# First products of 32 tokens by rows fetched by index, and dense weights scattered eight tokens at a time

## The chip, the core and the metric

The kernel runs on one core of a Trainium2 chip. A core has engines that work side by side, each with its own stream of instructions: TensorE (PE; its weight loads are listed apart as PEld), VectorE (DVE), ScalarE (ACT) and GpSimd (POOL). SyncE (SP) starts most transfers; 16 DMA engines carry them out between DRAM and the on-chip memories SBUF (operands) and PSUM (outcomes of TensorE). The metric is the device time of one run in microseconds (us). Before the change it was 1877.42 us, the median of 3 runs from 1877.06 to 1878.47.

## The reference, cut to what matters

One block of a hybrid network works on 512 tokens of 1024 features, with 16 meta tokens ahead of them: a norm, a recurrent branch and an attention branch, their gated sum with a residual, a second norm, and then a layer of 16384 small experts, of which every token takes 8 heads x 16 = 128. The change lies in that layer:

```python
def one_chunk(xt):                                   # 128 tokens
    q = (xt @ w_q).reshape(BLOCK, PEER_HEADS, PEER_QDIM)
    s1 = jnp.einsum('chd,nd->chn', q[..., :half], keys1)
    s2 = jnp.einsum('chd,nd->chn', q[..., half:], keys2)
    t1, i1 = lax.top_k(s1, PEER_TOPK)
    t2, i2 = lax.top_k(s2, PEER_TOPK)
    cand = (t1[..., :, None] + t2[..., None, :])     # 16 x 16 pairs of a head
    cidx = (i1[..., :, None] * PEER_NKEYS + i2[..., None, :])
    ts, sel = lax.top_k(cand, PEER_TOPK)             # the 16 best pairs
    idx = jnp.take_along_axis(cidx, sel, axis=-1)
    g = jax.nn.softmax(ts, axis=-1)
    act = jax.nn.gelu(jnp.einsum('chkd,cd->chk', u[idx], xt))
    return jnp.einsum('chk,chkd->cd', g * act, v[idx])
```

So a token's outcome is the sum over its 128 experts of weight x gelu(u[expert] . x) x v[expert]. The tables u and v have 16384 rows of 1024 numbers each. A last norm follows.

## The kernel before

The 512 tokens are four chunks of 128, taken in the order 1, 2, 3, 0 (`ORDER`). A float32 product is made of three products of split operands (`mm3`, L180 to 183): high by high, high by low, low by high, where ScalarE makes the high part (L155) and VectorE the low part (L156) of a weight tile (`wload`).

Chunk 0 goes by index: GpSimd fetches for each of 128 choices the 128 rows of u that the tokens want (`fetch`, L902), VectorE multiplies them by the tokens and sums each row (L913), and the same is done with v (L922).

Chunks 1 to 3, 384 tokens, go densely. For each of 128 blocks of 128 experts, `dense_products` makes `a` = u . x with 8 x 3 products of 384 columns, `gelu` makes `act` of it on ScalarE (L820), `stage` multiplies it by the dense softmax weights (`gt`, read from DRAM `gd`) and `dense` makes 18 products `y` of 512 columns with v, which sum up in PSUM over all blocks. First products run `LAG` = 41 blocks ahead of second products: block 0 within the mixing, 1 to 38 beside the choice and the scatter (`first_ahead`), and from block 39 on in the dense stage, where a step j holds the first products of block j + 41 and the second of block j. There a scheduler keeps VectorE's instructions in program order; elsewhere it places an instruction when its operands and a free buffer are there, earlier program order first. Pools with few buffers (`bufs`) tell when a transfer or an instruction can begin.

The dense weights come out of `scatter` (L843 to 881), once for each dense chunk. Its inputs are the choice's outcome `efx` (index) and `gate` (weight) of the chunk (`choose`, L757 to 815, nearly all on VectorE). After three transposes (`sct`) it goes four tokens at a time: VectorE makes `hb` (one-hot of the block, L868) and `hot` (one-hot of the expert within its block, L870); ScalarE scales three of four tokens' `hb` to `wj` (L875) and VectorE the fourth (L877); TensorE multiplies `hot` by `wj` into PSUM `sc` (L878); ScalarE copies `sc` to `stg` (L879), which holds 32 tokens. Every 32 tokens SyncE sends `stg` to `gd` (L881). The copy's loop is

```python
A.copy(stg[:, :, t4:t4 + 4].rearrange("p j t -> p t j"), o.rearrange("p (t j) -> p t j", t=4))
```

that is, it reads PSUM in order and writes with a distance of 32 numbers. The program's order (L883 to 890) is: key scores; choice of chunk 1; then three times a scatter in step with the next choice; each with its share of the blocks of `first_ahead`, by the table `ahead`.

Of the kernel before, what the change touches and what calls it, by code (L numbers as in the profile page):

```python
# [8 lines left out]
F32 = mybir.dt.float32  # L9
# [10 lines left out]
P = 128  # L20
D = 1024
NK = 8            # 128-row pieces of D_MODEL
NM = 16           # meta tokens
# [4 lines left out]
NH = 16           # attention heads  # L28
SCALE = 96.0 ** -0.5
PH = 8            # PEER heads  # L30
TOPK = 16
NS = PH * TOPK    # chosen experts of a token
NCAND = 50        # pairs (a, b) of ranks with (a + 1) * (b + 1) <= 16
NEG = -3.0e38
BIG = 1.0e30
# The pair of rank k (from 0) has (a + 1) * (b + 1) <= k + 1: blocks (a0, na, b0, nb) of pairs, by the
# group of four ranks that they can first have.
# [5 lines left out]
CO = (3, 0, 2, 1)    # chunks of queries of a pair of heads: the two sizes of the probabilities in turn  # L43
NJ = 128          # blocks of 128 experts
LAG = 41          # blocks that the first product runs ahead of the second
TS = 32           # tokens of a piece of the dense weights
JG = 4            # blocks of a load of the dense weights
# How the experts of a chunk are computed. Chunk 0: rows of both tables fetched by index.
# Chunks 1 to 3: products with both whole tables, times the dense softmax weights.
NDC = 3  # L50
ORD = (mybir.EngineType.DVE,)
SCA = 3           # tokens of four that ScalarE scales
LT = 2            # blocks of the first product between the two phases
GE = 6            # steps by which the fetches of rows end early
GA = ((0, 2), (2, 5))          # gate tiles that are computed between those of the recurrent branch
# [3 lines left out]
DT = NDC * P      # tokens of the dense chunks  # L59

# columns of the packed per-feature vectors
# [7 lines left out]
class in_order:  # L69
    """Keeps the instructions of the given engines that are traced within in the order of the program."""  # L70
# [22 lines left out]
def now(gen):  # L93
    """Runs a generator through; what it returns."""
    while True:
        try:
            next(gen)
        except StopIteration as e:
            return e.value
# [7 lines left out]
def interleave(*gens):  # L107
    """Runs generators in step, by the share of each that is done."""
# [10 lines left out]
def hybrid_block_kernel(ctx: ExitStack, tc, hT, x, win, wkr, vecs, wgate, wrnn, watt, wuq, wukv, wout,  # L119
# [9 lines left out]
    xn2d = dram.tile([P, D], F32, name="xn2d")  # L129
# [515 lines left out]
    def norm2(pos, c):  # L645
# [8 lines left out]
        if c == 0:  # L654
            nc.sync.dma_start(xn2d, t)
# [427 lines left out]
```

## Time and profile before

| | before |
|---|---|
| median of 3 runs | 1877.42 us (1877.06 to 1878.47) |
| profiled execution, its span | 1876.3 us |
| TensorE busy | 1821.0 us (97%) |
| VectorE busy | 1470.3 us (78%) |
| ScalarE busy | 981.4 us (52%) |
| GpSimd busy | 356.4 us (19%) |
| DMA, mean | 208 GB/s, 390.34 MB in all |

The trace is of one execution; its span is from its first to its last instruction, and 1.1 us lie between the span and the median of the runs. A busy share is a mean over stages with different limits, so the table below the change lists the stages apart: 553 to 688 us key scores, 688 to 717 the first choice, 717 to 967 the scatters and the other choices, 967 to 1697 the dense stage with both products, 1697 to 1822 its end with second products alone. Busy time of TensorE counts its matmuls with ends that are modelled, since they overlap.

### The profile page before, as it was taken

How to read it: one execution, taken by the hardware profiler on the slowest of the kernel's cores; microseconds unless marked ns; L12 is line 12 of the kernel's file. 1: busy time of each engine (PE TensorE's matmuls, PEld its weight loads, DVE VectorE, ACT ScalarE, POOL GpSimd, SP SyncE). 2: the span in 40 equal slices, each digit the busy share in tenths (PEclk: the TensorE clock that was granted, in tenths of full speed). 3: DMA queues.
4: the chain of work that ended last, by engine and by line, in shares of the span. 5: the costliest groups of instructions: out<-in, count | busy, mean ns of one | idle time of the engine just before them, and what ended most of it. 6: DMA issues, size and time to landing. Idle time of an engine off the chain costs nothing.

```text
span 1876.3 us, 28456 instructions
## 1 busy us (share of the span) xinstructions
PE 1821.0 (97%) x9731; PEld 1600.0 (85%) x9731; DVE 1470.3 (78%) x3280; ACT 981.4 (52%) x1915; POOL 356.4 (19%) x295
## 2 busy tenths in 40 slices
PE   8999999999999999999999999999999999999997
PEld 7888778877788888888899999998999999998886
DVE  7787677777546999898858788787887888887775
ACT  5778576766334337999963333333333333333343
POOL 0100000000100000000014344344444444443310
PEclk9999999999999999999999999999999999999999
DMA  5333212112733223454569999989998899988764
GB/s 162 92 101 104 74 54 66 62 55 85 241 113 129 85 85 130 144 194 158 189 225 348 321 318 340 326 300 322 324 334 313 304 331 321 343 309 280 266 223 152
DMA packets 181602, 390.34 MB, mean 208 GB/s; under 512 B 16593, under 2 KB 68305, under 8 KB 179921
## 3 DMA queue, kind: packets, MB, share of 16 engines
q1 hardware_dynamic: 141632, 245.97, 38.9%
q0 software_dynamic: 39536, 142.00, 21.8%
q8 instruction: 76, 1.25, 0.3%
q14 instruction: 70, 0.57, 0.1%
q10 hardware_dynamic: 288, 0.56, 0.1%
HBM read 353.44 MB, written 34.08 MB: 207 GB/s over the span
## 4 chain that ended last, share of the span: by engine, by line
PE 73%; ACT 10%; DMA 6%; DVE 6%; issue 3%; POOL 0%; DVEq 0%; ACTq 0%; SPq 0%; POOLq 0%
PE y L183 8%; PE y L182 8%; PE y L181 8%; PE a L183 7%; PE a L182 7%; PE a L181 7%; ACT stg L879 4%; PE q L181 2%; PE q L182 2%; PE wgr_ps L228 2%; PE q L183 2%; PE wga_ps L228 2%; PE wgn_ps L228 2%; PE sc L878 2%; ACT wj L875 2%
## 5 line engine op out<-in xcount | busy, mean ns | idle before, releaser
L183 PE MATMUL a<-xdh,ut_l 128*128 128x384 f32 x1024 | 346.3, 338 | 4.3 <-DVE ut_l L156 4.3
L181 PE MATMUL a<-xdh,ut_h 128*128 128x384 f32 x1024 | 348.1, 340 | 0.7 <-ACT act L820 0.5
L182 PE MATMUL a<-xdl,ut_h 128*128 128x384 f32 x1024 | 345.7, 338 | 0.3 <-DVE xdl L156 0.3
L155 ACT CAST ut_h<-ut_w 128x512 fp32r<-128x512 f32 x256 | 159.2, 622 | 330.3 <-DMA ut_w<-in_peer_uT_dram 281.7
L183 PE MATMUL y<-vh,cl 128*128 128x512 f32 x768 | 300.6, 391 | 0.0
L182 PE MATMUL y<-vl,ch 128*128 128x512 f32 x768 | 300.3, 391 | 0.0
L181 PE MATMUL y<-vh,ch 128*128 128x512 f32 x768 | 299.0, 389 | 1.3 <-ACT ch L155 1.3
L902 POOL DMA_INDIRECT u<-in_peer_u_dram,eidx x128 | 162.7, 1271 | 682.9 <-DMA gt<-gd 458.5
L902 POOL DMA_INDIRECT v<-in_peer_v_dram,eidx x128 | 175.2, 1369 | 262.6 <-DVE acc L922 233.6
L156 DVE TENSOR_TENSOR ut_l<-ut_w,ut_h 128x512 fp32r<-128x512 f32 x256 | 170.5, 686 | 52.2 <-ACT ut_h L155 51.7
L183 PEld LDWEIGHTS a<-xdh,ut_l 128*128 128x128 f32 x1024 | 193.0, 188 | 5.2 <-DVE ut_l L156 5.0
L181 PEld LDWEIGHTS a<-xdh,ut_h 128*128 128x128 f32 x1024 | 193.0, 188 | 4.7 <-ACT act L820 0.9
L182 PEld LDWEIGHTS a<-xdl,ut_h 128*128 128x128 f32 x1024 | 192.9, 188 | 3.9 <-DVE xdl L156 0.5
L156 DVE TENSOR_TENSOR vl<-vr,vh 128x1024 fp32r<-128x1024 f32 x128 | 157.6, 1232 | 40.6 <-ACT vh L155 40.4
L155 ACT CAST ch<-gt 128x384 fp32r<-128x384 f32 x128 | 65.7, 513 | 233.8 <-DVE gt L952 228.8
L922 DVE SCALAR_TENSOR_TENSOR acc<-v,coef,acc 128x1024 f32<-128x1024 f32 x128 | 164.1, 1282 | 11.3 <-DMA v<-in_peer_v_dram,eidx 9.2
L183 PEld LDWEIGHTS y<-vh,cl 128*128 128x128 f32 x768 | 144.1, 188 | 30.6 <-DVE cl L156 0.3
L181 PEld LDWEIGHTS y<-vh,ch 128*128 128x128 f32 x768 | 144.2, 188 | 30.0 <-ACT ch L155 2.1
L182 PEld LDWEIGHTS y<-vl,ch 128*128 128x128 f32 x768 | 144.1, 188 | 28.4
L913 DVE SCALAR_TENSOR_TENSOR jk<-u,xn 128x1024 bf16<-128x1024 f32 x128 | 156.5, 1222 | 14.7 <-DMA u<-in_peer_u_dram,eidx 12.2
L155 ACT CAST vh<-vr 128x1024 fp32r<-128x1024 f32 x128 | 133.7, 1045 | 31.7 <-PE y L183 26.9
L156 DVE TENSOR_TENSOR cl<-gt,ch 128x384 fp32r<-128x384 f32 x128 | 71.5, 559 | 80.9 <-ACT ch L155 80.9
(349 smaller groups left out, 3569.2 us busy)
## 6 DMA issues: line engine op xcount, KB each, us to landing
ut_w<-in_peer_uT_dram SPq DMA_DIRECT2D x256, 256.0 KB, 6.2
vr<-in_peer_v_dram SPq DMA_DIRECT2D x128, 512.0 KB, 6.4
gd<-stg SPq DMA_DIRECT2D x12, 2048.0 KB, 7.3
gt<-gd SPq DMA_DIRECT2D x96, 256.0 KB, 6.9
wq_w<-in_wq_dram SPq DMA_DIRECT2D x32, 256.0 KB, 2.7
wxr_w<-in_win_dram SPq DMA_DIRECT2D x16, 256.0 KB, 2.7
wgr_w<-in_win_dram SPq DMA_DIRECT2D x16, 256.0 KB, 2.8
wga_w<-in_win_dram SPq DMA_DIRECT2D x16, 256.0 KB, 2.6
```

Of the source, the lines that this page charges most:

```text
L155: A.copy(dst_hi, src)
L156: V.tensor_sub(dst_lo, src, r32(dst_hi))
L181: TE.matmul(o, lh, rh, start=first, stop=False)
L182: TE.matmul(o, lh, rl, start=False, stop=False)
L183: TE.matmul(o, ll, rh, start=False, stop=last)
L228: TE.matmul(o[:m, :n], lhs, rhs[:, k, t0:t0 + n], start=k == 0 and i == 0, stop=k == NK - 1 and i == 2)
L875: A.activation(wj[:, u, :], hb[:, :, u], AF.Copy, scale=gt_[:, t0 + u:t0 + u + 1])
L878: TE.matmul(o[:, u * P:(u + 1) * P], hot[:, u, :], wj[:, u, :], start=True, stop=True)
L879: A.copy(stg[:, :, t4:t4 + 4].rearrange("p j t -> p t j"), o.rearrange("p (t j) -> p t j", t=4))
L902: G.indirect_dma_start(out=t, out_offset=None, in_=src, in_offset=bass.IndirectOffsetOnAxis(ap=eidx[:, s:s + 1], axis=0))
L913: V.scalar_tensor_tensor(jk, t, 1.0, xn2, op0=OP.mult, op1=OP.mult, accum_out=coef[:, s:s + 1])
L922: V.scalar_tensor_tensor(acc, t, coef[:, s:s + 1], acc, op0=OP.mult, op1=OP.add)
```

## The change

The last 32 tokens of chunk 3 leave the dense first products: `a` has 352 columns (`DA`) in place of 384, and so do `act` and the product with `gt`. For these tokens u . x is made of rows fetched by index: 32 fetches of 128 rows (32 tokens x 4 groups of choices on the partitions), each with one multiply-and-sum on VectorE (`early_rows`), and `early_coef` multiplies gelu of the outcome into `gate` before scatter 2 takes it. The tokens' input goes through DRAM (`xnid`) to lie on four groups of partitions. Second products stay as they were. The rows' tiles `ue` are in the buffers of v's tiles (`vr`).

Since scatter 2 wants these rows, chunk 3 is chosen first. The order is now: key scores; choice of chunk 3; choice of chunk 1 with 6 rows; scatter 0 with the choice of chunk 2 and 10 rows; scatter 1 with 16 rows; `early_coef`; scatter 2 with the choice of chunk 0. The table `ahead` gives 4 blocks of first products to the first choice, 5 to the second, and 10, 9 and 10 to the scatters (before: 7 to the choice, 9, 10 and 12 to the scatters).

The scatter goes eight tokens at a time. `hb` and `hot` have 1024 columns, all eight `wj` are made by ScalarE, `hot` and `wj` are in the buffers of v's parts (`vh`, `vl`), the products come one step later than their operands, and the copy to `stg` runs over the 128 blocks with the four tokens innermost. The diff leaves out comments that were taken away and so moved the line numbers.

```diff
-SCA = 3           # tokens of four that ScalarE scales
+SG = 8
...
+NI = 32
+CI = ORDER[NDC - 1]
+DA = DT - NI
...
+    xnid = dram.tile([NI, D], F32, name="xnid")
...
+        if c == CI:
+            nc.sync.dma_start(xnid, t[P - NI:, :])
...
-            mm3(o[:, :DT], *wsl(w, k), xdh[:, k, :DT], xdl[:, k, :DT], k == 0, k == NK - 1)
+            mm3(o[:, :DA], *wsl(w, k), xdh[:, k, :DA], xdl[:, k, :DA], k == 0, k == NK - 1)
...
-        a = actp.tile([P, DT], F32, tag="act", bufs=LAG + 1, name=f"act{j}")
-        A.activation(a, o[:, :DT], AF.Gelu_apprx_tanh)
+        a = actp.tile([P, DA], F32, tag="act", bufs=LAG + 1, name=f"act{j}")
+        A.activation(a, o[:, :DA], AF.Gelu_apprx_tanh)
...
-        for q in range(P // TS):
-            stg = sp_.tile([P, NJ, TS], F32, tag="stg", bufs=1, name=f"stg{gi}_{q}")
-            for t4 in range(0, TS, 4):
-                o = mm2(f"sc{gi}_{q}_{t4}")
-                t0 = q * TS + t4
-                hb = sp_.tile([P, P, 4], BF16, tag="hb", bufs=2, name=f"hb{gi}_{t0}")
-                V.tensor_tensor(hb, iota4, blk[:, t0:t0 + 4].unsqueeze(1).to_broadcast([P, P, 4]), op=OP.is_equal)
-                hot = sp_.tile([P, 4, P], F32, tag="hot", bufs=2, name=f"hot{gi}_{t0}")
-                V.tensor_tensor(hot, iota.unsqueeze(1).to_broadcast([P, 4, P]),
-                                it[:, t0:t0 + 4].unsqueeze(2).to_broadcast([P, 4, P]), op=OP.is_equal)
-                wj = sp_.tile([P, 4, P], F32, tag="wj", bufs=2, name=f"wj{gi}_{t0}")
+
+        def products(t0, hot, wj, stg):
+
+            q, t8 = divmod(t0, TS)
+            for h in range(0, SG, 4):
+                o = ps.tile([P, 512], F32, tag="s", bufs=3, name=f"sc{gi}_{t0 + h}") if h else mm2(f"sc{gi}_{t0}")
                 for u in range(4):
-                    if u < SCA:
-                        A.activation(wj[:, u, :], hb[:, :, u], AF.Copy, scale=gt_[:, t0 + u:t0 + u + 1])
-                    else:
-                        V.tensor_scalar(wj[:, u, :], hb[:, :, u], gt_[:, t0 + u:t0 + u + 1], None, op0=OP.mult)
-                    TE.matmul(o[:, u * P:(u + 1) * P], hot[:, u, :], wj[:, u, :], start=True, stop=True)
-                A.copy(stg[:, :, t4:t4 + 4].rearrange("p j t -> p t j"), o.rearrange("p (t j) -> p t j", t=4))
-                yield
-            nc.sync.dma_start(gd[gi, q], stg)
-
-    ahead = [1 + (LAG - LT - 1) * n // 72 for n in (0, 0, 14, 32, 50, 72)]
+                    TE.matmul(o[:, u * P:(u + 1) * P], hot[:, h + u, :], wj[:, h + u, :], start=True, stop=True)
+                A.copy(stg[:, :, t8 + h:t8 + h + 4], o.rearrange("p (t j) -> p j t", t=4))
+            if t8 + SG == TS:
+                nc.sync.dma_start(gd[gi, q], stg)
+
+        last = None
+        for t0 in range(0, P, SG):
+            if t0 % TS == 0:
+                stg = sp_.tile([P, NJ, TS], F32, tag="stg", bufs=1, name=f"stg{gi}_{t0 // TS}")
+            hb = sp_.tile([P, SG // 4, P, 4], BF16, tag="hb", bufs=2, name=f"hb{gi}_{t0}")
+            V.tensor_tensor(hb, iota4.unsqueeze(1).to_broadcast([P, SG // 4, P, 4]),
+                            blk[:, t0:t0 + SG].rearrange("p (h t) -> p h t", t=4).unsqueeze(2)
+                            .to_broadcast([P, SG // 4, P, 4]), op=OP.is_equal)
+
+            hot = r32(vp.tile([P, D], F32R, tag="vh", bufs=2, name=f"hot{gi}_{t0}")).rearrange("p (t e) -> p t e", t=SG)
+            V.tensor_tensor(hot, iota.unsqueeze(1).to_broadcast([P, SG, P]),
+                            it[:, t0:t0 + SG].unsqueeze(2).to_broadcast([P, SG, P]), op=OP.is_equal)
+            wj = r32(vp.tile([P, D], F32R, tag="vl", bufs=2, name=f"wj{gi}_{t0}")).rearrange("p (t e) -> p t e", t=SG)
+            for u in range(SG):
+                A.activation(wj[:, u, :], hb[:, u // 4, :, u % 4], AF.Copy, scale=gt_[:, t0 + u:t0 + u + 1])
+            yield
+            if last:
+                products(*last)
+            last = (t0, hot, wj, stg)
+            yield
+        products(*last)
+
+
+    xni = sp_.tile([P, D], F32, name="xni")
+    uix = sp_.tile([P, NI], I32, name="uix")
+    ud = sp_.tile([P, NI], F32, name="ud")
+    ct = sp_.tile([P, NS], F32, name="ct")
+    own = slice(P - NI, P)
+
+    def early_setup():
+        for g in range(P // NI):
+            nc.sync.dma_start(xni[g * NI:(g + 1) * NI, :], xnid)
+            V.tensor_copy(uix[g * NI:(g + 1) * NI, :], efx[CI][own, g * NI:(g + 1) * NI])
+
+    def early_rows(s0, s1):
+        for s in range(s0, s1):
+            t = vp.tile([P, D], F32, tag="vr", bufs=VB, name=f"ue{s}")
+            G.indirect_dma_start(out=t, out_offset=None, in_=peer_u,
+                                 in_offset=bass.IndirectOffsetOnAxis(ap=uix[:, s:s + 1], axis=0))
+            jk = sp_.tile([P, D], BF16, tag="jke", bufs=1, name=f"jke{s}")
+            V.scalar_tensor_tensor(jk, t, 1.0, xni, op0=OP.mult, op1=OP.mult, accum_out=ud[:, s:s + 1])
+            yield
+
+    def early_coef():
+        A.activation(ud, ud, AF.Gelu_apprx_tanh)
+        for g in range(P // NI):
+            V.tensor_copy(ct[own, g * NI:(g + 1) * NI], ud[g * NI:(g + 1) * NI, :])
+        V.tensor_mul(gate[CI][own, :], gate[CI][own, :], ct[own, :])
+
+    NA = LAG - LT
+    ahead = [1 + (NA - 1) * n // 72 for n in (0, 0, 8, 18, 36, 54, 72)]
     ga = [first_ahead(a, b) for a, b in zip(ahead, ahead[1:])]
     na_ = [b - a for a, b in zip(ahead, ahead[1:])]
     interleave((key_scores(), 17), (ga[0], na_[0]))
-    interleave((choose(0, ORDER[0]), 11), (ga[1], na_[1]))
-    for i in range(3):
-        c = ORDER[i]
-        interleave((scatter(i, gate[c], efx[c]), 33), (choose(i + 1, ORDER[i + 1]), 11), (ga[2 + i], na_[2 + i]))
+    interleave((choose(NDC - 1, CI), 11), (ga[1], na_[1]))
+    early_setup()
+    interleave((choose(0, ORDER[0]), 11), (early_rows(0, 6), 6), (ga[2], na_[2]))
+    interleave((scatter(0, gate[ORDER[0]], efx[ORDER[0]]), 33), (choose(1, ORDER[1]), 11), (early_rows(6, 16), 10),
+               (ga[3], na_[3]))
+    interleave((scatter(1, gate[ORDER[1]], efx[ORDER[1]]), 33), (early_rows(16, NI), NI - 16), (ga[4], na_[4]))
+    early_coef()
+    interleave((scatter(2, gate[CI], efx[CI]), 33), (choose(3, ORDER[3]), 11), (ga[5], na_[5]))
...
-        V.tensor_mul(gj, gj, acts.pop(j).rearrange("p (c q t) -> p c q t", c=NDC, q=P // TS))
+        ga_ = gj.rearrange("p c q t -> p (c q) t")[:, :DA // TS]
+        V.tensor_mul(ga_, ga_, acts.pop(j).rearrange("p (g t) -> p g t", t=TS))
```

The first place is VectorE's stream at the end of the first choice. Before, the choice's outcome (`efx1`) is followed by the indices of scatter 0 (`ei0`), the start of choice 2 (`work2`), block 9's parts (`ut9`) and the one-hots of scatter 0:

```order
L846 CAST ei0_7639<-efx1_81 128x128
L762 TENSOR_SCALAR work2_7655<-work2_7655 128x8x16
L847 TENSOR_SCALAR ei0_7639<-ei0_7639 128x128
L767 TENSOR_TENSOR work2_7655<-tv1_6188 128x8x16
L848 TENSOR_SCALAR ei0_7639<-ei0_7639 128x128
L767 TENSOR_TENSOR work2_7655<-tv1_6188 128x8x8
L850 CAST ff0_7643<-ei0_7639 128x256
L767 TENSOR_TENSOR work2_7655<-tv1_6188 128x8x5
L156 TENSOR_TENSOR ut9_l0_7665<-ut9_w0_7662,ut9_h0_7664 128x512
L156 TENSOR_TENSOR ut9_l512_7671<-ut9_w512_7668,ut9_h512_7670 128x512
L868 TENSOR_TENSOR hb0_0_7703<-iota4_6199,blk0_7649 128x512
L870 TENSOR_TENSOR hot0_0_7705<-iota_73,it0_7651 128x512
```

After, the first choice is that of chunk 3; its last sum is followed by the casts of its indices (`uix`), the start of choice 1 and the products with the rows `ue0` and on (`jke`), with rows left out here between the second casts and block 7's parts:

```order
L812 TENSOR_REDUCE efx3_84<-oh3_3_7518 128x8x4
L767 CAST work1_7536<-ti0_6193 128x256
L912 CAST uix_6204<-efx3_84 32x32 x4
...
L160 TENSOR_TENSOR ut7_l0_7617<-ut7_w0_7614,ut7_h0_7616 128x512
L160 TENSOR_TENSOR ut7_l512_7623<-ut7_w512_7620,ut7_h512_7622 128x512
L920 SCALAR_TENSOR_TENSOR jke0_7545,ud_6205<-ue0_7543,xni_6203 128x1024
L793 MAX ts1_7653<-work1_7536 128x8 x2
L794 MAX_INDEX sel1_7654<-ts1_7653,work1_7536 128x8
L920 SCALAR_TENSOR_TENSOR jke1_7592,ud_6205<-ue1_7590,xni_6203 128x1024
```

The one-hots of scatter 0 come at the end of choice 1, behind block 11's parts, in one instruction for eight tokens:

```order
L160 TENSOR_TENSOR ut11_l0_7882<-ut11_w0_7879,ut11_h0_7881 128x512
L160 TENSOR_TENSOR ut11_l512_7888<-ut11_w512_7885,ut11_h512_7887 128x512
L773 TENSOR_TENSOR work2_7868<-tv1_6190 128x8x4
L885 TENSOR_TENSOR hb0_0_7919<-iota4_6201,blk0_7862 128x1024
L890 TENSOR_TENSOR hot0_0_7921<-iota_74,it0_7864 128x1024
L885 TENSOR_TENSOR hb0_8_7932<-iota4_6201,blk0_7862 128x1024
L890 TENSOR_TENSOR hot0_8_7934<-iota_74,it0_7864 128x1024
```

So a second choice, three more blocks' parts and the first rows have moved in ahead of scatter 0 on VectorE.

The second place is ScalarE within scatter 0, where `wj` scales one-hots and `stg` copies out of PSUM. Before:

```order
L879 COPY stg_0_7701<-sc_0_8_7732 128x4x128
L875 ACTIVATE wj_12_7795<-hb_12_7791,gt_7653 128x128 x3
L820 ACTIVATE act_7788<-a_7763 128x384
L875 ACTIVATE wj_16_7810<-hb_16_7806,gt_7653 128x128 x2
L879 COPY stg_0_7701<-sc_0_12_7790 128x4x128
L875 ACTIVATE wj_16_7810<-hb_16_7806,gt_7653 128x128
L875 ACTIVATE wj_20_7825<-hb_20_7821,gt_7653 128x128 x3
L879 COPY stg_0_7701<-sc_0_16_7805 128x4x128
L155 CAST ut_h_7872<-ut_w_7870 128x512
```

After:

```order
L894 ACTIVATE wj_0_7923<-hb_0_7919,gt_7866 128x128 x8
L894 ACTIVATE wj_8_7936<-hb_8_7932,gt_7866 128x128 x8
L159 CAST ut_h_7961<-ut_w_7959 128x512
L826 ACTIVATE act_7990<-a_7965 128x352
L876 COPY stg_0_7918<-sc_0_7992 128x128x4
L876 COPY stg_0_7918<-sc_4_7998 128x128x4
L894 ACTIVATE wj_16_8008<-hb_16_8004,gt_7866 128x128 x8
L876 COPY stg_0_7918<-sc_8_8017 128x128x4
L876 COPY stg_0_7918<-sc_12_8023 128x128x4
```

Of four tokens' scalings three stood on ScalarE, now four do, in groups of eight; the copies stand in pairs behind them, and the dimensions of the copy's loop have changed places.

## Rows read from the trace of the kernel before

**Rows 1.** Windows: start:end, us, each engine's busy us, TensorE clock, DMA share, GB/s.
```profile
553.00:688.00 135.00, 131.15 (x667) 111.38 (x665) 110.25 (x568) 54.10 (x93) 0.00 (x0) 1.00 0.30 100
688.00:717.00 29.00, 27.57 (x150) 27.57 (x151) 28.66 (x125) 12.55 (x21) 0.00 (x0) 0.94 0.38 119
717.00:967.00 250.00, 231.34 (x1514) 214.79 (x1513) 215.76 (x693) 231.44 (x495) 0.00 (x0) 1.00 0.47 164
967.00:1697.00 730.00, 728.67 (x3688) 663.36 (x3687) 590.58 (x804) 263.96 (x439) 306.44 (x238) 1.00 0.93 323
1697.00:1822.00 125.00, 124.56 (x549) 102.66 (x549) 92.96 (x112) 47.66 (x61) 31.50 (x19) 1.00 0.79 262
```

**Rows 2.** Timeline of TensorE in a dense step: start us, us, operation.
```profile
1040.77 0.33 PE L181 MATMUL a<-xdh,ut_h 128*128 128x384 f32 x1
...
1044.96 0.39 PE L181 MATMUL y<-vh,ch 128*128 128x512 f32 x1
...
1049.08 0.33 PE L181 MATMUL a<-xdh,ut_h 128*128 128x384 f32 x1
```

**Rows 3.** Chain of waits: start us, us, group; 264 columns, then 512.
```profile
116.20 8.21 PE wxr_ps L228 x68
...
152.24 16.68 PE wgr_ps L228 x72
```

**Rows 4.** Windows: the dense stage's first 60 us, and its rest.
```profile
980.00:1040.00 60.00, 60.00 (x304) 54.43 (x303) 49.77 (x78) 21.77 (x35) 25.86 (x21) 1.00 0.98 349
1040.00:1697.00 657.00, 656.50 (x3320) 597.41 (x3319) 535.49 (x719) 237.44 (x395) 276.30 (x214) 1.00 0.92 321
```

**Rows 5.** Waits, 967 to 1375: engine, line, releaser, us, times, longest.
```profile
ACT ut_h L155 <- DMA ut_w<-in_peer_uT_dram: 154.9, 50, 6.5
...
DVE jk L913 <- DMA u<-in_peer_u_dram,eidx: 12.2, 17, 1.8
```

**Rows 6.** Groups by line, VectorE, 688 to 717: count, busy, mean ns, idle before.
```profile
L156 DVE TENSOR_TENSOR ut_l<-ut_w,ut_h 128x512 fp32r<-128x512 f32 x13 | 8.8, 682 | 0.2 <-ACT ut_h L155 0.2
```

**Rows 7.** Page's groups and DMA issues: rows fetched by index.
```profile
L902 POOL DMA_INDIRECT u<-in_peer_u_dram,eidx x128 | 162.7, 1271 | 682.9 <-DMA gt<-gd 458.5
...
L913 DVE SCALAR_TENSOR_TENSOR jk<-u,xn 128x1024 bf16<-128x1024 f32 x128 | 156.5, 1222 | 14.7 <-DMA u<-in_peer_u_dram,eidx 12.2
...
u<-in_peer_u_dram,eidx POOLq DMA_INDIRECT x128, 7.4
```

**Rows 8.** Groups by line and shape, 688 to 967: the scatter.
```profile
L878 PE MATMUL sc<-wj,hot 128*128 128x128 f32 x768 | 109.6, 285 | 17.8 <-ACT wj L875 12.1 <-DVE hot L870 1.8 <-DVE wj L877 1.3
...
L879 ACT COPY stg<-sc 128x512 f32<-128x512 f32 x96 | 101.6, 1111 | 4.0 <-DMA gd<-stg 3.0 <-PE sc L878 0.6
...
L875 ACT ACTIVATE wj<-hb,gt 128x128 f32<-128x128 bf16 x288 | 98.2, 412 | 5.7 <-DVE hb L868 5.2
L878 PEld LDWEIGHTS sc<-wj,hot 128*128 128x128 f32 x768 | 97.8, 191 | 33.6 <-ACT wj L875 31.2 <-ACT stg L879 1.5
L870 DVE TENSOR_TENSOR hot<-iota,it 128x512 f32<-128x512 f32 x96 | 65.7, 684 | 2.7 <-PE sc L878 2.1
...
L868 DVE TENSOR_TENSOR hb<-iota,blk 128x512 bf16<-128x512 bf16 x96 | 39.7, 418 | 14.6 <-ACT wj L875 13.2 <-ACT blk L856 1.4
L877 DVE TENSOR_SCALAR wj<-hb,gt 128x128 f32<-128x128 bf16 x96 | 26.8, 279 | 0.3 <-ACT gt L860 0.3
```

**Rows 9.** Timeline of ScalarE within scatter 1: start us, us, operation, count.
```profile
860.80 1.01 ACT L875 ACTIVATE wj<-hb,gt 128x128 f32<-128x128 bf16 x3 [0.45 <-DVE hb L868]
...
866.90 2.94 ACT L879 COPY stg<-sc 128x512 f32<-128x512 f32 x3 [0.49 <-DMA gd<-stg]
```

**Rows 10.** Groups by line, ScalarE, 553 to 688: a copy between contiguous places.
```profile
L747 ACT COPY scs<-sc 128x512 f32<-128x512 f32 x16 | 9.4, 588 | 0.9 <-PE sc L745 0.7
```

## The prediction

> **What bounds the kernel now.** I first read the busy time of each engine in stretches, then what ends the waits in those stretches. [rows 1] divide the run from 553 us to 1822 us: key scores, one choice of experts (688 to 717), the three scatters of the dense weights with the three other choices (717 to 967), the dense stage with both products (967 to 1697), and its end with second products alone. In the dense stage TensorE works 728.67 of 730 us, so whatever a step of it saves is saved at the end. A step lasts 1049.08 - 1040.77 = 8.31 us [rows 2]: 24 first products (`a`, 384 columns) in 1044.96 - 1040.77 = 4.19, or 0.1746 each, and 18 second products (`y`, 512 columns) in 4.12. The stretch 717 to 967 is another case: TensorE is busy 231.3, ScalarE 231.4 and VectorE 215.8 of 250 us, so three engines hold one another up, each with a little slack. In 688 to 717 VectorE alone is full, 28.66 of 29 us. The execution's span is 1876.3 us and the median of the runs 1877.42, so 1.1 us lies around it; the sums below are differences and hold for both.
>
> **The change part by part.** *Shorter first products.* No row has 352 columns, so I take a line through neighbours: 264 columns take 8.21 / 68 = 0.1207 us each and 512 columns 16.68 / 72 = 0.2317 [rows 3]. From 264 to 384 that is 0.45 ns a column, from 384 to 512 0.42 (with 4.12 / 18 for `y`) to 0.45. So 32 columns are worth 0.0136 to 0.0144 us, 24 products 0.33 us a block. Of the 128 blocks 89 (39 to 127) have their first products in the dense stage: 89 x 0.33 = -29 us. The other 39 lie earlier, where the saving counts only as TensorE's load. Bounds: 0, if something other than TensorE then sets the step, and -31.
>
> *What is late next in the dense stage.* Its transfers run at 0.92 of the DMA engines' time and 321 GB/s; in the 60 us after the stage begins they ran at 0.98 and 349 [rows 4]. A step of 7.98 us with the same bytes wants 321 x 8.31 / 7.98 = 334 GB/s, between the two. ScalarE already waits 154.9 us for pieces of u in 967 to 1375, at most 6.5 at a time, and VectorE 12.2 us in 17 waits for rows fetched by index [rows 5]: TensorE, busy nearly all the time there, shows that the buffers hide these waits now. With 4% less time per step some of it will show. I price that at +4 us, between 0 and the whole 29.
>
> *One choice more ahead of the first scatter.* Now the choice of chunk 3, then the choice of chunk 1, stand before scatter 0, where one choice stood. A choice costs VectorE 28.66 - 8.8 = 19.9 us, the 8.8 being 13 subtractions for the parts of u [rows 1, 6]. Two choices 39.8; 22 such subtractions (11 blocks now stand there) x 0.68 = 14.9; about 7 of the 32 rows. A row costs VectorE 1.22 us by its row, 1.27 with the read of the sum [rows 7]: 8.9. Together 63.6. A fetched row lands 7.4 us after its issue and POOL needs 1.27 us to issue one [rows 7]; POOL is idle in this stretch [rows 1], three buffers let fetches run ahead, and a product that waits has choice instructions of 0.2 us queued behind it in VectorE's order. I add 4 us: 68, against 29 before: +39 us. TensorE has 11 x 3.86 = 42 us to do in it, so it idles there, which it did not before. Bounds: 60 (no wait) and 80 (each of the seven rows waits some 2 us).
>
> *The scatters.* TensorE: its 231.3 us held 38 - 27.57 / 4.19 = 31.4 blocks = 132 us, so the rest, mostly 768 scatter passes, was 100. Now 27 blocks x 3.86 + 100 = 204. VectorE: 215.8, less 26.8 for the `wj` that go to ScalarE [rows 8], less 19.9 for the choice that went ahead, less 4.4 blocks x 2 x 0.68 = 6, plus 25 rows x 1.27 = 32: 195; `hb` and `hot` (39.7 and 65.7 us [rows 8]) come in half as many instructions of twice the width, which is 0 to -8 more. ScalarE: 231.4, plus 96 more `wj`. Three took 1.01 us [rows 9], so eight in a row 2.5; 48 x 2.5 = 121 against 98.2 [rows 8]: +23. Less 4.4 blocks of casts and a gelu, -7, and one choice's two table loads, -3.
>
> Everything then hangs on the 96 copies `stg<-sc` from PSUM. Before, each read PSUM in a run and wrote one number every 128 bytes: 1111 ns, 101.6 us in all [rows 8]; three in a row took 2.94 us [rows 9]. The same size between contiguous places took 588 ns [rows 10]. The new copy writes runs of four numbers, but reads PSUM with a hop of 512 bytes from number to number. No row shows a hopping read of PSUM by ScalarE. Nearest is the contiguous copy on one side (pairs at 0.48 + 0.59 = 1.07 us, 48 x 1.07 = 51, or -50), the copy of before on the other (0). I take -50, because the row of before has its hop on the write side alone, and this is what goes: 231 + 23 - 10 - 50 = 194. [...]
>
> With 204, 195 and 194 us of work where there were 231, 216 and 231, and the same slack, the stretch takes 250 x 204 / 231.3 = 221 us: -29. That the products follow a step later than their operands may remove slack; stage buffers of one (`stg` before its DMA) keep some. I leave it.
>
> *Small parts.* The last 32 rows of chunk 3's input go to DRAM and back (128 KB, four copies) beside the choice of experts, where DMA is at 0.38 [rows 1]: nothing. The copies of indices are four small casts ahead of choice 1 on VectorE, 0.5 us, in the 4 above. The 32 coefficients join ahead of scatter 2, behind the last row; if that is late, scatter 2's transpose of the weights waits while blocks of `a` remain: nothing, at most 5.
>
> **Sum.** -29 + 4 + 39 - 29 = -15, that is 1877.4 - 15 = 1862 us.
>
> **The rivals.** *A, ScalarE's copies stay at 1.1 us (slower).* Place: `stg<-sc` in 717 to 967. Then ScalarE has 231 + 23 - 10 = 244 us to do, and the scatters take 250 x 244 / 231.4 = 264 instead of 221: -29 + 4 + 39 + 14 = +28, 1905 us. For it: a hop cost the old copy half its speed; against: that hop was in SBUF. The point from which it decides: the net is zero where the scatters take 236, that is with 218 us on ScalarE, which a copy of about 0.8 us gives. Halfway, 1884.
>
> *B, the dense step does not get shorter (slower).* Transfers at 0.92 and ScalarE's waits for u speak for it [rows 4, 5], the 349 GB/s reached after 980 against. The step stays 8.31, the -29 and the +4 go, and +10 from the two stages before is left: 1887; with half the step's gain 1875.
>
> *C, eight tokens at a time free the scatter of its waits.* PE's weight load waits 31.2 us for `wj` in 688 to 967 [rows 8]; products that come a step behind their operands would not. The stretch then ends with TensorE's own 204 plus 4: -42 instead of -29, 1849 us. Against: the single `stg`, and VectorE and ScalarE at 194 nearly as full.
>
> **How the numbers follow.** Forecast 0.47 (1854 to 1872 by its own bounds), A 0.30 (1880 to 1906, by how fast the copy is), B 0.13 (1873 to 1889), C 0.10 (1846 to 1853). A difference under 0.2%, 3.8 us, can't be told from none here. Faster: 0.47 + 0.10 + 0.02 of B = 0.59. Same: 0.02 of A and 0.04 of B = 0.06. Slower: 0.28 + 0.07 = 0.35. The range leaves out the lower half of C and A's slowest end: 1849 to 1902.
>
> **What would show it.** Steps of `a` to `a` in the dense stage at 7.95 to 8.05 us say that the 29 is there; 8.2 or more says B. `stg<-sc` near 0.59 us mean, 0.48 in a row, says forecast or C; 0.9 or more says A. VectorE full for 64 to 70 us between the end of the key scores and the first `hot` confirms the 39. From the first `hot` to the first step of the dense stage: 221 forecast, 264 A, 208 C. The forecast is wrong if TensorE's clock falls while it idles in the two choices (it was 0.94 in 688 to 717 [rows 1]) and stays low, or if the row products hold VectorE so that `hb` comes late.

## The result and the profile after

The changed kernel takes 1897.38 us, the median of 4 runs (1896.7 to 1901.88), beside 1877.95 for the kernel before: ratio 1.0097, 95% interval 1.0074 to 1.012. It is slower; 1862 was forecast. The span of the profiled execution is 1895.7 us, 19.4 more than the 1876.3 of before. One execution each of three kernels below took far longer than the others of its kernel (2072.97 us in `b352`, 8302.64 in `b352b`, 2225.84 in `bcrb4`), and all times and ratios here leave these out.

These are busy times in stretches of the changed kernel, to be held against [rows 1] (start:end, length, busy time of TensorE, its weight loads, VectorE, ScalarE and GpSimd, then TensorE's granted clock, DMA share, GB/s). The bounds follow its stages: two choices from 688 to 754, scatters to 985, the dense stage to 1715.

```profile
553.00:688.00 135.00, 128.83 (x659) 108.97 (x657) 110.63 (x570) 50.69 (x89) 0.00 (x0) 1.00 0.27 89
688.00:754.00 66.00, 46.97 (x211) 43.41 (x212) 63.09 (x266) 20.00 (x35) 12.29 (x10) 0.77 0.47 148
754.00:985.00 231.00, 211.03 (x1454) 202.85 (x1454) 191.63 (x430) 210.38 (x578) 29.89 (x22) 0.97 0.64 227
985.00:1715.00 730.00, 708.44 (x3699) 636.49 (x3698) 588.00 (x805) 264.32 (x442) 303.06 (x238) 1.00 0.93 324
1715.00:1840.00 125.00, 121.40 (x528) 99.89 (x527) 90.71 (x110) 45.36 (x58) 32.06 (x19) 0.99 0.79 261
```

The row of the dense stage holds the surprise: TensorE, which was busy 728.67 of 730 us, now has 21.6 us of gaps in a stretch of the same length at 324 GB/s, where it was 323.

Three marks of the timelines (the first `hb` on VectorE, the first and the last `y` on TensorE) split both spans, in us:

| | before | after | difference | forecast |
|---|---|---|---|---|
| start to first `hb` | 719.5 | 753.5 | +34.0 | +39 |
| first `hb` to first `y` | 259.2 | 244.9 | -14.2 | -29 |
| first `y` to last `y` | 888.2 | 888.5 | +0.3 | -25 |
| last `y` to end | 9.5 | 8.7 | -0.8 | 0 |
| span | 1876.3 | 1895.7 | +19.4 | -15 |

A step that runs undisturbed is as short as forecast. In the timeline of TensorE after (start, duration, operation), against [rows 2]:

```profile
1106.58 0.32 PE L185 MATMUL a<-xdh,ut_h 128*128 128x352 f32 x1
...
1110.44 0.39 PE L185 MATMUL y<-vh,ch 128*128 128x512 f32 x1
...
1114.52 0.32 PE L185 MATMUL a<-xdh,ut_h 128*128 128x352 f32 x1
```

24 first products of 352 columns take 1110.44 - 1106.58 = 3.86 us, to the hundredth the estimate of 4.19 - 0.33, and the step 7.94. But of the 86 steps from the first `y` of one to the first `y` of the next, 21 are longer than the median of 7.96 us by 0.2 to 3.7 us, 26 us in all, many of them four steps apart: the mean step is 8.26. What TensorE waits for shows in the waits of the changed kernel from 1100 to 1400 us (engine, line, releaser: total us, times, longest):

```profile
ACT ut_h L159 <- DMA ut_w<-in_peer_uT_dram: 118.2, 37, 7.3
...
PEld a L185 <- ACT act L826: 14.3, 11, 2.4
PE a L185 <- ACT act L826: 9.7, 9, 1.9
...
DVE jk L964 <- DMA u<-in_peer_u_dram,eidx: 8.0, 11, 2.4
```

The same waits in the kernel before, 1100 to 1400 us:

```profile
ACT ut_h L155 <- DMA ut_w<-in_peer_uT_dram: 118.2, 36, 6.5
...
PEld a L181 <- ACT act L820: 0.9, 1, 0.9
PE a L181 <- ACT act L820: 0.5, 1, 0.5
```

ScalarE waited as long for u before, and TensorE hardly noticed; now the waits reach TensorE. One such stall, from the changed kernel's timelines of SyncE's issues (SPq), VectorE, ScalarE and TensorE in order of time:

```profile
1216.87 2.10 SPq L996 DMA_DIRECT2D gt<-gd  x3
...
1220.53 1.29 DVE L160 TENSOR_TENSOR ut_l<-ut_w,ut_h 128x512 fp32r<-128x512 f32 x2
...
1221.24 0.95 SPq L170 DMA_DIRECT2D ut_w<-in_peer_uT_dram  x2
...
1230.48 0.62 ACT L159 CAST ut_h<-ut_w 128x512 fp32r<-128x512 f32 x1 [6.47 <-DMA ut_w<-in_peer_uT_dram]
1231.01 0.46 ACT L826 ACTIVATE act<-a 128x352 f32<-128x352 f32 x1
1231.03 1.29 DVE L160 TENSOR_TENSOR ut_l<-ut_w,ut_h 128x512 fp32r<-128x512 f32 x2
...
1231.52 0.43 PE L185 MATMUL a<-xdh,ut_h 128*128 128x352 f32 x1 [1.95 <-ACT act L826]
```

Read it as a chain. VectorE's `ut_l` is the last reader of two raw tiles; SyncE refills them 0.7 us after its start, behind three loads of `gt`, and the piece is there 9.2 us later. ScalarE stands at that piece's cast, with the gelu `act` behind it in its stream although its `a` was long complete; TensorE wants the PSUM tile that `act` is to free. So the wait named as ScalarE's is a transfer's, and the transfer's is that of a raw tile of which there are three for two pieces a step. One round of this loop, from VectorE's read to its next, took 0.71 us to the issue, 9.24 to the cast and 0.55 to the next read, 10.5 us in all. With the median landing of a piece in 1100 to 1400 us,

```profile
ut_w<-in_peer_uT_dram SPq DMA_DIRECT2D x72, 256.0 KB, 6.7
```

the same round would take 0.71 + 6.7 + 0.55 = 7.96 us (an estimate): shorter than the step of before, 8.31, and no shorter than the new one. Since two tiles are read and refilled in a row (the `x2`), three of them hold one such round at a time.

ScalarE's copy is fast. Groups of the scatter after, from 680 to 1010 us (count, busy us, mean ns, idle before), against [rows 7, 8]:

```profile
L894 ACT ACTIVATE wj<-hb,gt 128x128 f32<-128x128 bf16 x384 | 120.8, 424 | 4.4 <-DVE hb L885 3.2 <-PE sc L875 1.2
...
L890 DVE TENSOR_TENSOR hot<-iota,it 128x1024 f32<-128x1024 f32 x48 | 58.3, 1218 | 7.9 <-PE sc L875 7.9
...
L876 ACT COPY stg<-sc 128x512 f32<-128x512 f32 x96 | 50.8, 604 | 6.9 <-DMA gd<-stg 5.1 <-PE sc L875 1.7
...
L920 DVE SCALAR_TENSOR_TENSOR jke<-ue,xni 128x1024 bf16<-128x1024 f32 x32 | 39.0, 1219 | 11.4 <-DMA ue<-in_peer_u_dram,uix 11.3
```

604 ns in place of 1111, 50.8 us in place of 101.6; 120.8 us of scalings where 121 were worked out, 39.0 us of row products (without the reads of their sums) where 41 were with them.

### The profile page after: what moved, and what is told of

Its sections match the earlier page's. It is cut to its first block, busy times and chain, and to the rows that moved or that the text cites. A ratio compares the mean times of both kernels' runs of the same rounds, so it can differ in the third digit from the quotient of the medians.

```text
span 1895.7 us, 28480 instructions
## 1 busy us (share of the span) xinstructions
PE 1796.2 (95%) x9731; PEld 1571.6 (83%) x9731; DVE 1477.5 (78%) x3161; ACT 964.6 (51%) x2012; POOL 395.7 (21%) x327
## 4 chain that ended last, share of the span: by engine, by line
issue 18%; PE 11%; DMA 11%; POOL 6%; ACT 4%; DVE 3%; DVEq 0%; POOLq 0%; ACTq 0%; SPq 0%
DMA ut_w<-in_peer_uT_dram 5%; POOL v L953 4%; PE y L185 3%; PE y L186 3%; PE y L187 3%; DMA v<-in_peer_v_dram,eidx 3%; POOL u L953 2%; ACT wj L894 2%; DMA u<-in_peer_u_dram,eidx 1%; DVE ut_l L160 1%; ACT stg L876 1%; DMA ue<-in_peer_u_dram,uix 1%; PE a L185 1%; PE a L187 1%; PE a L186 1%
## 5 line engine op out<-in xcount | busy, mean ns | idle before, releaser
L185 PE MATMUL a<-xdh,ut_h 128*128 128x352 f32 x1024 | 343.8, 336 | 29.0 <-ACT act L826 20.6
L187 PE MATMUL a<-xdh,ut_l 128*128 128x352 f32 x1024 | 341.7, 334 | 20.7 <-DVE ut_l L160 19.5
L186 PE MATMUL a<-xdl,ut_h 128*128 128x352 f32 x1024 | 337.2, 329 | 0.3 <-DVE xdl L160 0.3
L185 PEld LDWEIGHTS a<-xdh,ut_h 128*128 128x128 f32 x1024 | 198.3, 194 | 43.8 <-ACT act L826 29.7
L187 PEld LDWEIGHTS a<-xdh,ut_l 128*128 128x128 f32 x1024 | 198.0, 193 | 28.4 <-DVE ut_l L160 27.8
L186 PEld LDWEIGHTS a<-xdl,ut_h 128*128 128x128 f32 x1024 | 198.9, 194 | 3.0 <-DVE xdl L160 0.5
L187 PEld LDWEIGHTS y<-vh,cl 128*128 128x128 f32 x768 | 144.6, 188 | 31.2 <-DVE cl L160 0.8
L964 DVE SCALAR_TENSOR_TENSOR jk<-u,xn 128x1024 bf16<-128x1024 f32 x128 | 156.5, 1223 | 14.2 <-DMA u<-in_peer_u_dram,eidx 11.7
```

What stands on the lines that cost most here:

```text
L185: TE.matmul(o, lh, rh, start=first, stop=False)
L186: TE.matmul(o, lh, rl, start=False, stop=False)
L187: TE.matmul(o, ll, rh, start=False, stop=last)
L964: V.scalar_tensor_tensor(jk, t, 1.0, xn2, op0=OP.mult, op1=OP.mult, accum_out=coef[:, s:s + 1])
```

## The experiments

All were measured in 3 rounds against the kernel before on the same chip. `b352`, `b352b`, `b352r4` and `arb4nr` leave out the first products of 32 tokens and `afew` leaves out transfers: they price work and are no kernels to use. Readings within a run are of one execution.

**The columns alone** (`b352`, and `b352b` again for its stages). The kernel before with

```diff
-            mm3(o[:, :DT], *wsl(w, k), xdh[:, k, :DT], xdl[:, k, :DT], k == 0, k == NK - 1)
+            mm3(o[:, :DA], *wsl(w, k), xdh[:, k, :DA], xdl[:, k, :DA], k == 0, k == NK - 1)
```

and `act` and the product with `gt` on 352 columns.

> The kernel before with first products, gelu and the product with the weights on 352 columns, and nothing else; the first products of 32 tokens are left out. Theory T1 (transfers pace the dense stage: a step moves the same bytes, some 320 GB/s x 8.31 us, and nothing shorter on TensorE helps): first y to last y stays at 886 to 889 us as before and after the change, total 1868 to 1878. Theory T2 (TensorE still sets the step, and the stalls in the changed kernel come from how it enters the stage or from its other edits): first y to last y about 860, total 1838 to 1850.

> The kernel before with 352 columns alone once more (the first products of 32 tokens are left out), for the stages. By the ring of three raw tiles: median step 7.95 to 7.97 us, but the 87 full steps take 718 to 726 us with stalls every fourth step, as in the changed kernel; total 1872 to 1878. If the stalls came with the change's other edits: full steps 693 to 700 us.

Measured: 1875.3 us, ratio 0.9974 (0.9958 to 0.9989), and 1872.47, ratio 0.9966 (0.9952 to 0.9981). In the second, the 86 steps take 709.6 us (710.0 in the changed kernel) with 21 stalls of 24.9 us in all, first `y` to last `y` 886.3 against 888.2. (The expectations count 87 full steps to the first `y` of block 88, which takes in one step of second products alone; by that count it is 720.3.) So 32 columns fewer, which are some 29 us of TensorE's work there, give 2 us in the dense stage by themselves; neither the rows nor the new scatter are to blame for that.

**One fetch in eight left out** (`afew`), the changed kernel with

```diff
-            t = fetch(peer_u, c, s, f"u{c}_{s}")
+            t = fetch(peer_u, c, s, f"u{c}_{s}") if s % 8 != 7 else t
```

and the same for v.

> The changed kernel, where one in eight of chunk 0's row fetches is left out in the dense stage (the row fetched before it is used twice, VectorE's work is the same). T1: a step moves 2.49 MB instead of 2.66, at 320 GB/s 7.8 us, so TensorE's 7.97 decides again: first y to last y 860 to 868 against 888, total 1868 to 1877. T2: no effect, 1893 to 1899.

Measured: 1876.85 us, 20.5 less than the changed kernel, ratio 0.9983 (0.9965 to 1.0), first `y` to last `y` 868.2. The numbers are T1's.

**Rows moved to the last steps** (`aw52`):

```diff
-            yield 1 if w is None else 4
+            yield 2 if w is None else 5
...
-        interleave((dense(), 4 * NJ - 3 * LAG), (chain(first_by_index(0), second_by_index(0, acc)), 2 * NS + 2 + GE))
+        interleave((dense(), 5 * NJ - 3 * LAG), (chain(first_by_index(0), second_by_index(0, acc)), 2 * NS + 2 + GE))
```

> The changed kernel with other shares of chunk 0's rows: 5 for a step with both products and 2 for one with second products alone, in place of 4 and 1, so that about 2.53 rows go with a full step in place of 2.69 and 41 instead of 28 with the last 41 steps. V: a full step moves 2.57 MB, at 320 GB/s 8.04 us in place of 8.31: the 87 full steps take 699 to 706 us instead of 722.6, the tail a few us more, total 1875 to 1884. R (tiles, not bytes): under half of that, 1887 to 1896.

Measured: 1872.31 us, ratio 0.9961 (0.9949 to 0.9974); the full steps take 700.0 us by the expectation's count. Also as theory V, that bytes are the limit, has it (the total is 3 us below its range). Both runs would have made V the story, but for the next.

**A fourth raw tile** (`arb4`), the changed kernel with

```diff
-WB, RB, GB, VB, XB = 3, 3, 4, 3, 1
+WB, RB, GB, VB, XB = 3, 4, 4, 3, 1
```

> The changed kernel with four raw tiles for weight pieces in place of three. Theory V (volume: the 320 GB/s of this mix is what transfers give, at 0.93 of the DMA engines' time): first y to last y stays at 885 to 889 us, total 1893 to 1899. Theory R (the ring: a piece of u lands about 7 us after its issue, 9 when the weights gt are loaded every fourth step, and three tiles for two pieces a step don't cover that): first y to last y 862 to 872, total 1871 to 1882.

Measured: 1863.23 us, ratio 0.9913 (0.9897 to 0.993), first `y` to last `y` 855.5, no step over 8.1 us: better than R's own range. A dense stretch of it:

```profile
995.00:1685.00 690.00, 689.13 (x3636) 627.66 (x3637) 582.23 (x801) 266.54 (x433) 310.43 (x238) 1.00 0.96 338
```

TensorE is full again and the same transfers run at 338 GB/s, so 320 was not what they can give. ScalarE's waits for u from 1100 to 1400 us fall from 118.2 to 48.4 us:

```profile
ACT ut_h L159 <- DMA ut_w<-in_peer_uT_dram: 48.4, 20, 5.5
```

By itself that fall says little, since before it was 118.2 with TensorE full; but the waits of TensorE for `act` are gone with it. V falls, R stands: the loop of three tiles set the pace. Fewer bytes (`afew`, `aw52`) help a loop as well, which is why they could not tell the two apart: in `afew` a piece of u landed after 6.3 us in place of 6.7 and a load of `gt` after 6.6 in place of 9.0 (medians, 1100 to 1400 us).

**Both, without rows and new scatter** (`b352r4`): the columns alone, and four raw tiles; `hot` goes to the buffers of v's parts for room.

> The kernel before with 352 columns (the first products of 32 tokens are left out) and four raw tiles, hot in the buffers of v's parts to make room. If the ring is the cause and not the rows or the new scatter: no stalls, full steps 690 to 697 us against 718 to 726 with three tiles, total 1838 to 1848. If bytes were the limit: like the three tiles, 1870 or more.

Measured: 1842.55 us, ratio 0.9803 (0.9775 to 0.9831), first `y` to last `y` 855.5. A dense stretch of `b352b` and then one of `b352r4`:

```profile
974.00:1694.00 720.00, 701.53 (x3646) 629.95 (x3646) 587.70 (x801) 259.43 (x434) 309.75 (x238) 1.00 0.93 325
```

```profile
976.00:1660.00 684.00, 683.92 (x3613) 623.37 (x3614) 579.54 (x797) 267.57 (x432) 305.20 (x235) 1.00 0.96 339
```

Together with `bcrb4` below (384 columns, four tiles) this makes four cases of the time from first `y` to last `y`, in us:

| | three raw tiles | four raw tiles |
|---|---|---|
| 384 columns | 888.2 (before) | 886.5 (`bcrb4`) |
| 352 columns | 886.3 (`b352b`) | 855.5 (`b352r4`) |

Each alone gives some 2 us. With the fourth tile the columns are worth 886.5 - 855.5 = 31 us there, the size that the forecast gave them.

**The scatter alone** (`b8`), all of the eight-token form in the kernel before, and **the turned copy alone** (`bcopy`):

```diff
-                A.copy(stg[:, :, t4:t4 + 4].rearrange("p j t -> p t j"), o.rearrange("p (t j) -> p t j", t=4))
+                A.copy(stg[:, :, t4:t4 + 4], o.rearrange("p (t j) -> p j t", t=4))
```

> The kernel before with the scatter in steps of eight tokens alone (384 columns, no row fetches, the order of before). From first hb to first y it took 259 us before, 245 in the changed kernel. If TensorE bounds these stages (231 us of work in 250), it can give no more than about 15: 243 to 250 here, total 1861 to 1870. If the waits between the three engines were the cost, about the forecast's 0.9 of the work of the busiest engine stays: 255 or more, total 1872 or more.

> The kernel before with only the copy out of PSUM turned round (runs of four numbers written, PSUM read with a hop); four tokens a step as before. The copy takes about 600 ns as in the changed kernel, ScalarE has 50 us less to do. If the copy is what the scatter's gain is made of: most of what the eight-token scatter alone gives, total 1863 to 1872. If the longer steps and the products one step late make it: 1875 to 1880, no gain.

The eight-token form holds the turned copy too. Measured: 1865.73 us, ratio 0.9914 (0.9885 to 0.9943), for the eight-token form; 1853.33, ratio 0.9848 (0.9818 to 0.9877), for the one line. From first `hb` to first `y` 241.0 and 234.4 against 259.2. I had expected the line to give no more than the whole. The copy's group in `bcopy`, 688 to 967 us, and the stretches from first `hb` to first `y` of before, of `bcopy` and of `b8`:

```profile
L879 ACT COPY stg<-sc 128x512 f32<-128x512 f32 x96 | 54.0, 588 | 9.7 <-PE sc L878 6.5 <-DMA gd<-stg 2.7
```

```profile
719.00:978.00 259.00, 240.14 (x1564) 223.72 (x1563) 217.63 (x689) 233.53 (x498) 2.66 (x2) 1.00 0.49 172
```

```profile
719.00:953.00 234.00, 230.48 (x1563) 222.67 (x1562) 213.59 (x689) 197.37 (x497) 2.84 (x2) 1.00 0.55 191
```

```profile
720.00:961.00 241.00, 230.32 (x1565) 226.34 (x1563) 190.35 (x497) 222.12 (x596) 2.72 (x3) 0.99 0.52 186
```

With the line alone TensorE is busy 230.48 of 234 us: nothing is left there. The eight-token form takes VectorE from 214 to 190 and gives it to ScalarE, 197 to 222, and TensorE waits 11 us.

**Four-token steps in the changed kernel** (`a4`): the loop of before with the turned copy, `hot` in the buffers of v's parts.

> The changed kernel with four-token steps again (three of four scalings on ScalarE, products at once), but the copy turned round as in the change. The four-token scatter with the turned copy took 234 us from first hb to first y in the kernel before, the eight-token one 241. If the eight-token form itself costs: 236 to 240 here against 245, total 1888 to 1893. If VectorE, which has rows to do as well, can't take back a quarter of the scalings: 245 to 255, total 1896 to 1908.

Measured: 1891.11 us, ratio 1.0054 (1.0037 to 1.0071); first `hb` to first `y` 237.0 against 244.9. In that stretch the eight-token form costs 7 to 8 us in either kernel (241.0 - 234.4, 244.9 - 237.0); of the whole time it is 12.4 and 6.3.

**The order of before ahead of scatter 0** (`aorder`):

```diff
-    interleave((choose(NDC - 1, CI), 11), (ga[1], na_[1]))
-    early_setup()
-    interleave((choose(0, ORDER[0]), 11), (early_rows(0, 6), 6), (ga[2], na_[2]))
...
+    interleave((choose(0, ORDER[0]), 11), (ga[1], na_[1]))
+    interleave((scatter(0, gate[ORDER[0]], efx[ORDER[0]]), 33), (chain(own_choice(), choose(1, ORDER[1])), 22), (ga[2], na_[2]))
...
```

where `own_choice` is chunk 3's choice and `early_setup`, all 32 rows go with scatter 1, and the table `ahead` is that of before.

> The changed kernel with the order of before ahead of scatter 0: the choice of chunk 1 alone, then scatter 0 with the choices of chunks 3 and 2, scatter 1 with all 32 rows, scatter 2 with the choice of chunk 0. The first hb comes at about 720 us again instead of 753. If the second choice costs because TensorE has too little to do beside it: first y at 975 to 986 instead of 998, total 1875 to 1886. If VectorE's work sets the stages either way: first y at 992 to 1000, total 1890 or more.

Measured: 1888.0 us, ratio 1.0051 (1.0029 to 1.0072); first `hb` at 722.5, first `y` at 987.2. Of the 31 us at the first mark 11 are left at the second, between the two theories.

**Without the early rows** (`arb4nr`), four raw tiles.

> The changed kernel with four raw tiles and without the early rows (fetches, products and their gelu left out; the order of choices and scatters is the same). It prices the rows in the stages ahead of the dense one, where the first hb came at 758 and the first y at 996 with them. If VectorE's 40 us of row products are what is late: first hb about 748, first y 960 to 975. If the order with two choices costs by itself, since TensorE idles there: first hb 748 to 753, first y 982 to 992.

Measured: 1839.68 us, ratio 0.9799 (0.9779 to 0.982); first `hb` at 743.7 against 758.0 in `arb4`, first `y` at 968.0 against 995.9. The same two stages of `arb4`, then of `arb4nr`:

```profile
688.00:758.00 70.00, 44.80 (x209) 41.24 (x210) 63.96 (x274) 19.73 (x34) 11.71 (x10) 0.77 0.44 139
758.00:996.00 238.00, 219.88 (x1517) 212.06 (x1516) 195.54 (x438) 215.63 (x590) 32.38 (x26) 0.97 0.68 240
```

```profile
688.00:744.00 56.00, 44.59 (x232) 41.26 (x233) 55.79 (x257) 21.51 (x38) 0.00 (x0) 0.91 0.27 90
744.00:968.00 224.00, 211.59 (x1492) 204.94 (x1491) 165.73 (x378) 212.01 (x583) 3.86 (x4) 0.98 0.53 192
```

The rows cost 14 us in the two choices, where VectorE is full without them, and 13 or 14 in the scatters, where it is not: 165.73 of 224 us busy without, 195.54 of 238 with. Their products in the same two stages of `arb4`, seven and then 25:

```profile
L920 DVE SCALAR_TENSOR_TENSOR jke<-ue,xni 128x1024 bf16<-128x1024 f32 x7 | 8.5, 1216 | 3.7 <-DMA ue<-in_peer_u_dram,uix 3.7
```

```profile
L920 DVE SCALAR_TENSOR_TENSOR jke<-ue,xni 128x1024 bf16<-128x1024 f32 x25 | 30.4, 1214 | 7.6 <-DMA ue<-in_peer_u_dram,uix 7.6
```

So 39 us of VectorE's work set the end back by 28: in the choices all of it and the waits for the rows besides, in the scatters under half. The run leaves out the fetches (16.8 MB) along with the products; it prices the rows as a whole, and how much of the 13 us in the scatters is VectorE's and how much the transfers' was not tried.

**Forms that might beat the turned copy.** `bcrb4` is the turned copy with four raw tiles in the kernel before. `bbest4` is the changed kernel with the order of `aorder`, four-token steps and four raw tiles; `aorb4` the same with eight-token steps; `b4a` like `bbest4` with all scalings on ScalarE.

> The kernel before with the turned copy and four raw tiles (hot in the buffers of v's parts): all 384 columns, no rows. The turned copy gave 1853 with 5 us of stalls in the full steps. The ring says that four tiles take these away and no more, since TensorE sets the step at 8.31: 1846 to 1851. If the fourth tile gave more than the stalls, the step would have to be shorter than 8.31: under 1844.

> The changed kernel with everything that the runs point to: order of before ahead of scatter 0 (choices of chunks 3 and 2 beside it), four-token steps with the turned copy, four raw tiles. If the gains add up (-9 for the order, -6 for the four-token steps, -34 for the fourth tile): 1844 to 1852, level with the kernel before with the turned copy. If VectorE, with rows, choices and a quarter of the scalings, is full beside scatters 0 and 1: first y at 985 or later, total 1853 or more.

> The changed kernel with the order of before ahead of scatter 0 and four raw tiles, eight-token steps as in the change. VectorE was busy 248 of 260 us with four-token steps in this order; with all scalings on ScalarE it has 26 us less. If VectorE's load sets it: first y at 983 to 988, total 1848 to 1854. If not: as with four-token steps, 995 or later, total over 1860.

> As the run before it, but with steps of four tokens, products at once and all four scalings on ScalarE. If the load of VectorE alone decides: like the eight-token steps in this order, first y 980 to 988, total 1845 to 1854. If four-token steps leave ScalarE and TensorE waiting for each other at every step: first y 990 or later, total 1856 or more.

Measured: 1855.47 us, ratio 0.9872 (0.9841 to 0.9902); 1865.19, 0.9928 (0.9901 to 0.9955); 1857.08, 0.9892 (0.9871 to 0.9914); 1861.83, 0.9909 (0.9886 to 0.9932). None is faster than `bcopy`. In `bcrb4`, expected at 1846 to 1851, the stalls are gone (first `y` to last `y` 886.5 against 892.4), but the first `y` comes 4 us later, 3 of them at the first `hb` already; why was not tried. The first `y` of the others comes at 997.6, 990.4 and 997.2 us: the second theory's place in `bbest4` and `b4a`, between the two in `aorb4`. `bbest4` from first `hb` to first `y` shows VectorE as the engine that sets the pace, and `aorb4`, without VectorE's scalings, shows none that does, and no gain in proportion:

```profile
721.00:998.00 277.00, 240.21 (x1565) 223.75 (x1564) 253.09 (x763) 201.71 (x501) 36.18 (x35) 0.96 0.65 229
```

```profile
721.00:990.00 269.00, 232.08 (x1564) 224.22 (x1563) 226.69 (x570) 222.93 (x598) 47.06 (x35) 0.94 0.66 235
```

## Why the prediction was wrong

Of the 34 us between forecast and measured span, 25 lie in the dense stage and 15 in the scatters; the choices gave 5 back.

- *Shorter first products, -29.* Right as a term: 3.86 us for 24 of them, a median step of 7.96, and 31 us once nothing else binds (`b352r4`).
- *What is late next, +4.* This is the step that failed. The forecast asked whether 334 GB/s is within what the DMA engines reach, and took TensorE's fullness before as a sign of cover. It is a sign that the cover was enough at 8.31 us, not of how much was over. ScalarE's 154.9 us of waits for u [rows 5] were the loop's, not idle time to spare: three raw tiles, each refilled only after VectorE has read it. The cost was about the whole 29 (first `y` to last `y` +0.3), the far end of the bounds, and rival B's outcome. Of the two things that B named, the transfers at 0.92 of their time were not the limit, since `arb4` ran the same ones at 338 GB/s, and the waits for u were the place. The sign that was to show the 29, steps of 7.95 to 8.05 us, came true for most of the steps and misled: the mean, 8.26, says B.
- *One choice more, +39.* Measured +34, within its bounds. VectorE was busy 63.09 us there, 63.6 forecast. Without the rows (`arb4nr`) the first `hb` comes 743.7 - 719.5 = 24 us later than before, for the second choice and three blocks' parts; the rest is rows. TensorE's clock fell there, one of the signs of being wrong, but did not stay low: 0.77, then 0.97 in the scatters and 1.00 in the dense stage.
- *The scatters, -29.* The mechanism was right and the size off: -14. ScalarE's copy took 604 ns as chosen, against rival A. But the rows were counted as load on an engine that is not the fullest, hence as free; they cost 13 us there. From first `hb` to first `y` it is 244.9 us in the changed kernel, 237.8 with the fourth tile (`arb4`, whose first `hb` comes 4.5 us later) and 224.4 without the rows too (`arb4nr`); the 250 us of [rows 1] are 259.2 by these marks, so that the 221 worked out is 230 here. The eight-token form, which I left at nothing, costs 7 to 8 us besides (`a4`, `b8`). And ScalarE's load was put at 194 us and was 210.38: the whole 50 us that the copies' group loses was taken off its busy time, but in `bcopy` that fell by 36 only (233.53 to 197.37) when the group fell by 47.6, since the times of its groups overlap (from 719 to 978 us of the kernel before they add up to 267 us, where ScalarE was busy 233.53).
- *Rival C* did not come as a time, though its mechanism did: the weight loads' wait for `wj` fell from 31.2 us [rows 8] to 6.5. In its place TensorE waited for `ut_l`, which VectorE makes. Waits from 754 to 985 us:

```profile
PEld a L187 <- DVE ut_l L160: 13.3, 14, 3.9
PEld sc L875 <- ACT wj L894: 6.5, 6, 2.5
```

- *The hopping read of PSUM.* No row of before showed one, so the -50 was my choice between the contiguous copy and the copy of before; the runs bear it out. With a hop of 512 bytes at every element of the read the copy took 588 ns in `bcopy`, as long as the contiguous copy [rows 10], and 604 in the changed kernel, in place of 1111.

The net at the first `y` is +19.8 us (978.6 to 998.4). By pairs of runs the turned copy gave -25 there (`bcopy`), the columns of the early blocks -5 (`b352b`), the rows +28 (`arb4nr`), the order with two choices ahead +11 (`aorder`, which moves the rows as well) and the eight-token form +8 (`a4`): +17, near the 19.8, though effects taken in different kernels need not add up. The dense stage gave nothing. The turned copy did not need the rest of the change: undone down to that one line, the kernel takes 1853.33 us.

## What to carry to other kernels

A full engine (here TensorE, 728.67 of 730 us at 8.31 us a step) says that its suppliers keep up at the present pace and nothing of the slack behind them (with a median step of 7.96 it had 21.6 us of gaps in as long a stretch): before pricing a shorter step, follow a supply loop around once (last reader, issue, landing, cast), count how many of its rounds the tiles allow at once, and hold that against the step. A run with fewer bytes does not tell a volume limit from a loop of too few tiles; a run with one tile more does (`arb4`, 855.5 us from first to last `y` in place of 888.5). And work that is moved to an engine below full load is not free where three engines hand on to each other: here 30 us of row products in the scatters came with 13 us more time.

## What the runs showed of the hardware

A hop of 512 bytes from element to element in PSUM cost ScalarE's copy nothing (588 ns in `bcopy` for 128x512, as contiguous), while with a hop of 128 bytes from number to number on the writing side, into SBUF, it took 1111 ns. TensorE's granted clock was 0.77 in the stretch with two choices and rows, where the engine was busy 47 of 66 us, 0.91 without the rows (`arb4nr`, 45 of 56 us), and 1.00 in the dense stage of before (728.67 of 730 us). The 0.77 is a mean of unequal parts: from 735 to 745 us the clock was 1.00, from 745 to 750 us, in which TensorE was busy 0.59 us, it was 0.82, and from 750 to 755 us 0.50. At what it falls was not tried.
